# A scan's first pair, fetched and fronted inside the projections that precede it

## Chip, cores and metric

One core of one Trainium2 chip runs the whole program. The metric is device time in microseconds (us), the median of several executions; a profile of one more execution gives the trace.

## What is computed

Two encoder layers over 512 tokens of width 1024, in float32. Each layer is a half-step SwiGLU feed-forward, a token mixer, and a second half-step feed-forward, each followed by a residual and a layer norm. The mixer of layer 0 is neighbourhood attention, that of layer 1 a bidirectional RWKV-7 scan, and the change lies at the border inside this second mixer, between its projections and its scan. Cut to what matters there:

```
xr, xw, xk, xv, xa, xg = (x + xx * mix[i] for i in range(6))
r = xr @ w_rkv[0];  k = xk @ w_rkv[1];  v = xv @ w_rkv[2]
decay = exp(-exp(-softplus(-wl) - 0.5))         # wl: w0 + tanh(xw @ w1) @ w2, for two directions z
a = sigmoid(a0 + (xa @ a1) @ a2)                # for two directions z
g = sigmoid(xg @ g1) @ g2
step: state = state * w_t + (state @ a_t) b_t + v_t k_t;  out = state @ r_t
return ((y + bonus) * g) @ w_out
```

## The kernel before

**Stages.** Three feed-forwards and the attention come first, then `rwkv_project` (the projections), then the scan (`Scan`), then the last feed-forward. Matmuls that need float32 precision are made of three passes over a high and a low part (`mm3`, L225 to L227); `split` makes the parts, the high one on ACT (L220) and the low one on DVE or POOL (L221).

**Projections.** `rwkv_project` keeps the raw activations of all tokens in one tile `xraw` (pool `xr`). `mixed(i)` makes the split mix for a projection, `raws(i, dst)` the unsplit mix, which goes to DRAM. `decays(z)` computes the log-decays of direction z (eight matmul groups, eight stores into `d_lw`). The last loop makes the gate: per channel block c six matmuls from `gh` and `ug`, one ACT copy out of PSUM (L628) and one store into `d_g`. Its results pass through eight slots of a ring. The matrix of receptances r is made for the first block alone; xr and xv go to DRAM for the scan to use.

**Scan.** Heads are worked in eight pairs hp, tokens in eight chunks, directions in z = 0, 1. `load(hp)` fetches k, the inverse norms iv and a2 of a pair. `front(hp, z)` fetches r and the log-decays `lw`, sums them over tokens with four matmuls against a triangular constant `tri` (L1212, into bank "a"), takes two exponentials (L1215, L1217), makes the second LoRA product with `ah` and `a2u` (mm3 in bank "a"), a tanh (L1222) and, on DVE, the scaled operands `ar` and `bk`. `grams(hp, z)` multiplies `bk` by `ar` for four chunks at a time (L1271), masks the product into a unit tile `xs` on DVE (L1276), and then, for each of two heads, copies three pieces of `xs` on ACT (`qd`, `qc`; L1280, L1282) and moves two halves by DMA:

```
nc.scalar.activation(p.qc[h * 64 : h * 64 + 32, us, :], x[r : r + 32, h, :, 0, 32:64], AF.Copy)
nc.sync.dma_start(az[own, h], x[own, h, :, 1, :])
nc.sync.dma_start(x[own, h], ar[hs, ss])
```

The last of these overwrites what the ACT copy reads, so it waits for that copy. `receptances` (thread "r") loads the eight blocks of xr (into `az` and two units `xs`), the weights of r for pair 1 (into a unit `xs`), the eight blocks of `xv`, then more weights, and computes r for pairs 1 to 7 in groups of eight matmul rows (L982, banks "y" and "m"). `outs` (thread "o", from slot 6 on) loads rows of `w_out` into tiles that have come free, `w[0]` to `w[7]`, and adds up the output projection of the first five pairs: steps for i = 0, 1, 2, 3, 4 in this order.

**Order.** In the scan PE, ACT and DVE run in the order in which the code issues their work, and a table `SEQ` interleaves the threads of each slot. In the projections only PE's order is that of the code; the other engines' is planned by a timeline model when the program is built. All DMAs go out from SP's queue, whose order is planned too. Slot -2 begins `g0 v f1 f1 f1 f1 f1 f1 g0 l g0 r r`: a gram group of (0, 0), then front (0, 1), then the first receptance steps.

**Pools.** `rwb` holds the scan's tiles and opens when the projections' pools close; `rwe` on the right holds those tiles (`EARLY_TAGS`) that must be free before the last slot.

Of the kernel before, what the change touches and what calls it, by code (L numbers as in the profile page):

```python
# [10 lines left out]
F32 = mybir.dt.float32  # L11
# [61 lines left out]
EARLY = 5  # L73
EARLY_TAGS = ("k", "iv", "r", "lw", "kz", "a2r", "a2u", "v", "vr", "qc", "qd", "zs", "qs", "tm")
DECAY = math.exp(-0.5)
# [23 lines left out]
class Trunk:  # L99
# [78 lines left out]
    def bank(self, tag="bank"):  # L178
        return self.ps.tile([P, 512], F32, name=tag, tag=tag, bufs=self.banks.get(tag))

# [388 lines left out]

    def rwkv_project(self, dram, xraw, w_rkv, w1, w2, a1, g1, g2, heads):  # L570

        nc = self.nc
        with self.pool("rwa") as pool:
            with self.behind(self.mid):
# [73 lines left out]
            with self.tc.manual_schedule(engines=MANUAL):  # L648
# [55 lines left out]
                u = self.load_cols(g1, 0)  # L704
                u2 = pool.tile([P, 2, ND, 32], F32R, name="g1b")
                raw = self.tmp()[:, : ND * 32].rearrange("p (c f) -> p c f", c=ND)
# [270 lines left out]
class Scan:  # L977
# [5 lines left out]

    def __init__(self, k, pool, dram, consts, a2, w_r, w_v, w_out):
        self.k, self.nc, self.pool, self.dram, self.a2, self.w_r, self.w_v, self.w_out = k, k.nc, pool, dram, a2, w_r, w_v, w_out
        nc = self.nc
        self.opened = ExitStack()
        early = self.early = self.opened.enter_context(k.pool("rwe", "right"))
        self.first = {}
        self.tri = early.tile([P, 2, P], F32, name="tri")  # L990
        self.mask = early.tile([P, 2, 2, CH], F32, name="mask")
        self.onesb = early.tile([P, P], F32, name="onesb")
        self.eye = consts["eye"]
        self.ah = early.tile([P, 2, S], F32R, name="ah")
        self.xv = pool.tile([P, ND, S], F32, name="xv")
        self.consts = consts
# [17 lines left out]
        self.free = list(range(NBUF))  # L1014
        self.taken, self.st, self.py = {}, {}, {}

# [3 lines left out]
    def tile(self, tag, shape, bufs=1, dtype=F32):  # L1020
        if tag in self.first:
            return self.first.pop(tag)
        pool = self.early if tag in EARLY_TAGS else self.pool
        return pool.tile(shape, dtype, name=tag, tag=tag, bufs=bufs)
# [54 lines left out]
    def run(self, late, lead, ln):  # L1079
        with self.k.tc.manual_schedule(engines=MANUAL_SCAN):  # L1080
            raw = self.tile("e", [P, S], 2)
            for dst, src in ((raw, self.dram["ah"]), (self.tri, self.consts["tri"])):
                self.nc.sync.dma_start(dst, src)
# [3 lines left out]
            for n in ("mask", "onesb"):  # L1087
                self.nc.sync.dma_start(getattr(self, n), self.consts[n])
            self.zs = []
# [90 lines left out]
    def load(self, hp):  # L1180
# [11 lines left out]
        k.split(p.a2u[:, 0], p.a2u[:, 1], raw)  # L1192
        p.pc = tile_("pc", [P, NC, 2], 4)
        p.qd = tile_("qd", [P, NU, 32], 2)
        p.qc = tile_("qc", [P, NU, 32], 2)
        p.az = self.az[hp % 3]
        p.units, p.ar, p.bk = [], [], []
        yield

    def front(self, hp, z):  # L1200
# [7 lines left out]
        lw = tile_("lw", [P, NT, P], 2)  # L1208
        nc.sync.dma_start(lw, self.dram["lw"][:, z, :, hp * P : (hp + 1) * P])
        pi = k.bank("a")  # L1210
# [11 lines left out]
        nc.scalar.activation(th, pa, AF.Tanh, scale=0.5, bias=k.col(C_A0H + z, hp))  # L1222
        ar = tile_("ar", [P, NC, 2, CH], 2)
        bk = tile_("bk", [P, NC, 2, CH], 2)
        at, rt = ar[:, way, 0, :], ar[:, way, 1, :]
# [14 lines left out]
        if z == 0:  # L1240
            nc.vector.scalar_tensor_tensor(p.iv, p.k, k.col(C_KKH, hp), p.iv, ALU.mult, ALU.mult)
        kz = tile_("kz", [P, S], 2)
        nc.scalar.activation(kz, th, AF.Identity, scale=k.col(C_KA1, hp), bias=k.col(C_KA2, hp))
# [219 lines left out]
    def outs(self):  # L1463
# [114 lines left out]
def trunk_kernel(tc, x, ffn_w_in, ffn_w_out, ln_g, ln_b, cols, w_qkv, b_qkv, bias, mask, w_o, b_o,  # L1578
                 w_rkv, w1, w2, a1, a2, g1, g2, rw_out, heads, tri, smask, onesb, eye, out):
    nc = tc.nc  # L1580
    with ExitStack() as ctx:
# [12 lines left out]
        with k.activations(), k.psum(bank=8), k.weights(3):  # L1594
# [11 lines left out]
            with ExitStack() as xs:  # L1606
                with k.behind(*k.last):
                    xraw = k.ffn(xT, ffn_w_in[1, 0], ffn_w_out[1, 0], 3, lambda: XRaw(k, xs.enter_context(k.pool("xr"))))
                k.store_x(grid(dram["x"]))
                k.rwkv_project(dram, xraw.x, w_rkv, w1, w2, a1, g1, g2, heads)  # L1610
        with ExitStack() as late:
            with k.pool("rwb") as pool:
                scan = Scan(k, pool, dram, dict(tri=tri, mask=smask, onesb=onesb, eye=eye), a2, w_rkv[0], w_rkv[2], rw_out)
                with k.psum(a=2, g=2, p=1, c=1, m=1, y=1):
# [78 lines left out]
```

## Time and profile before

| what | value |
|---|---|
| median of 3 runs | 2267.66 us (2266.18 to 2270.35) |
| the profiled execution, its own time | 2262.09 us |
| its span, its mean granted PE clock | 2260.3 us, 0.984 |
| PE, weight loads (PEld) busy | 2169.9 us (96%), 1707.2 us (76%) |
| DVE, ACT, POOL busy | 1084.6 us, 974.6 us, 1423.4 us |
| DMA queue of SP | 326.58 MB, 45.9% of 16 engines' span |

The projections' last matmul ends at about 1442.6 us of the span and the last feed-forward follows the scan at about 1900 us. PE is busy nearly everywhere; what matters is where it is not. In the rows that follow, each row of a timeline has the start, the duration, the engine, line, operation, output and inputs, the count of merged instructions and, in brackets, the idle time before it with the instruction that ended it.

### The profile page before, as it was taken

The page shows a single profiled execution, that of the slowest core. Times are in us where ns is not written, and L with a number is a line of the kernel's source. Part 1 is how long each engine was busy: PE and PEld are TensorE (multiplying, and loading weights), DVE is VectorE, ACT ScalarE, POOL GpSimd, SP SyncE. Part 2 cuts the span into 40 slices and gives each one's busy share as a digit, 9 for nine tenths or more (in the row PEclk, how much of TensorE's full clock was granted, in tenths as well). Part 3 has the DMA queues.
Part 4 walks back from the last instruction along what each step waited for, and adds up shares of the span by engine and source line. Part 5 has one row for each costly group of instructions (what it writes and reads, how often), then busy time and mean ns, then how long its engine had stood idle before and what let it go on. Part 6 is the DMA issues. An engine that isn't in the chain of part 4 may idle for free. (4 is left out here: it accounts for less than half of the span.)

```text
span 2260.3 us, 35130 instructions
## 1 busy us (share of the span) xinstructions
PE 2169.9 (96%) x13784; PEld 1707.2 (76%) x13784; DVE 1084.6 (48%) x1549; ACT 974.6 (43%) x1706; POOL 1423.4 (63%) x1237
## 2 busy tenths in 40 slices
PE   8999999999999999999999988799999898999998
PEld 7888878887888888788888775435666556888886
DVE  2333356376423333743333698435787535233346
ACT  4333335376333333533333436336777533333334
POOL 6878855554487886588777433144776712888763
PEclk9999999999999999999999999899999999999999
DMA  7444463432344445354444534864444542444443
GB/s 204 143 149 145 140 214 101 134 89 91 103 140 149 144 141 181 123 176 140 140 140 134 192 122 143 275 165 132 134 125 119 181 149 85 158 144 140 145 168 121
DMA packets 350497, 328.82 MB, mean 145 GB/s; under 512 B 48458, under 2 KB 277450, under 8 KB 350332
## 3 DMA queue, kind: packets, MB, share of 16 engines
q1 hardware_dynamic: 350332, 326.58, 45.9%
q8 instruction: 108, 1.77, 0.3%
q14 instruction: 57, 0.47, 0.1%
HBM read 262.26 MB, written 47.74 MB: 137 GB/s over the span
## 5 line engine op out<-in xcount | busy, mean ns | idle before, releaser
L221 POOL TENSOR_TENSOR w<-raw,w 128x1024 fp32r<-128x1024 f32 (+2 forms) x203 | 501.5, 2472 | 253.6 <-ACT w L220 240.1
L226 PE MATMUL bank<-xT,w 128*128 128x512 f32 x1416 | 551.8, 390 | 1.7 <-DVE xT L221 1.7
L225 PE MATMUL bank<-xT,w 128*128 128x512 f32 x1416 | 552.9, 390 | 0.0
L227 PE MATMUL bank<-xT,w 128*128 128x512 f32 x1416 | 551.5, 389 | 0.0
L220 ACT ACTIVATE w<-raw 128x1024 fp32r<-128x1024 f32 x207 | 218.4, 1058 | 327.9 <-POOL ts L768 138.0
L422 DVE SCALAR_TENSOR_TENSOR ar<-bank,tmp 128x512 f32<-128x512 f32 x88 | 60.9, 692 | 580.7 <-PE bank L227 566.2
L226 PEld LDWEIGHTS bank<-xT,w 128*128 128x128 f32 x1416 | 266.1, 188 | 56.6 <-DVE xT L221 2.6
L227 PEld LDWEIGHTS bank<-xT,w 128*128 128x128 f32 x1416 | 266.0, 188 | 54.9
L225 PEld LDWEIGHTS bank<-xT,w 128*128 128x128 f32 x1416 | 266.0, 188 | 54.0
L797 PE MATMUL bank<-w,ring 128*128 128x512 f32 x864 | 201.5, 391 | 11.0 <-DVE w L221 10.1
L797 PEld LDWEIGHTS bank<-w,ring 128*128 128x128 f32 x864 | 161.6, 188 | 48.3 <-DVE w L221 13.1
L797 PE MATMUL bank<-wx,an 128*128 128x512 f32 x792 | 187.3, 389 | 0.0
L1360 POOL TENSOR_TENSOR tm<-qs,zs 128x126 f32<-128x126 f32 (+22 forms) x248 | 105.5, 425 | 125.7 <-DVE qs L1353 77.3
L797 PEld LDWEIGHTS bank<-wx,an 128*128 128x128 f32 x792 | 148.8, 188 | 30.8
L221 POOL TENSOR_TENSOR wx<-ra,wx 128x512 fp32r<-128x512 f32 x132 | 166.8, 1291 | 3.5 <-ACT wx L220 2.4
L221 DVE TENSOR_TENSOR ring<-ar,ring 128x1024 fp32r<-128x1024 f32 x44 | 130.0, 2955 | 76.0 <-ACT ring L220 75.9
L420 ACT ACTIVATE tmp<-bank 128x512 f32<-128x512 f32 x88 | 52.6, 598 | 225.8 <-PE bank L227 225.7
L221 POOL TENSOR_TENSOR ring<-raw,ring 128x1024 fp32r<-128x1024 f32 x28 | 69.7, 2499 | 105.6 <-ACT ring L220 105.6
L1362 POOL TENSOR_TENSOR zs<-zs,tm 128x126 f32<-128x126 f32 (+22 forms) x248 | 112.2, 452 | 19.4
L221 POOL TENSOR_TENSOR w<-late,w 128x1024 fp32r<-128x1024 f32 x28 | 71.3, 2547 | 75.9 <-ACT w L220 68.9
L220 ACT ACTIVATE wx<-ra 128x512 fp32r<-128x512 f32 x132 | 82.9, 633 | 72.4 <-PE bank L797 67.9
L225 PE MATMUL bank<-xT,ring 128*128 128x256 f32 (+1 forms) x352 | 104.5, 304 | 9.5 <-ACT xT L220 3.4
(285 smaller groups left out, 3730.5 us busy)
## 6 DMA issues: line engine op xcount, KB each, us to landing
raw<-in_ffn_w_in_dram SPq DMA_DIRECT2D x176, 512.0 KB, 3.7
ra<-in_ffn_w_out_dram SPq DMA_DIRECT2D x44, 1024.0 KB, 4.9
late<-d_late SPq DMA_DIRECT2D x30, 512.0 KB, 6.0
late<-in_ffn_w_out_dram SPq DMA_DIRECT2D x28, 512.0 KB, 4.4
raw<-in_w_qkv_dram SPq DMA_DIRECT2D x24, 512.0 KB, 3.8
d_late<-ts SPq DMA_DIRECT2D x44, 256.0 KB, 3.1
d_late<-ra SPq DMA_DIRECT2D x44, 256.0 KB, 2.0
xs<-ar SPq DMA_DIRECT2D x64, 128.0 KB, 2.3
```

The costliest lines, as they stand in the source:

```text
L220: self.hi = self.nc.scalar.activation(h, raw, AF.Copy).ins
L221: self.lo = (eng or self.nc.vector).tensor_tensor(l, raw, h.bitcast(F32), ALU.subtract).ins
L225: nc.tensor.matmul(out, wh, xh, start=start, stop=False)
L226: nc.tensor.matmul(out, wh, xl, start=False, stop=False)
L227: nc.tensor.matmul(out, wl, xh, start=False, stop=stop)
L420: nc.scalar.activation(s, pg, AF.Silu)
L422: nc.vector.scalar_tensor_tensor(raw[:, 3:7:3] if j else raw[:, 0:8:7], halves_of(pu), 0.5, halves_of(s), ALU.mult, ALU.mult)
L797: self.nc.tensor.matmul(acc, lhs, u[:, i], start=bool(first) and m == 0, stop=last and m == 2, skip_group_check=more)
L1360: nc.gpsimd.tensor_tensor(tv, qs[:, s, 0:s].rearrange("p (a o) -> p a o", o=1).broadcast_to([P, s, n]), zs[:, s : s + 1, c0:].broadcast_to ...
L1362: nc.gpsimd.tensor_tensor(zs[:, 0:s, c0:], zs[:, 0:s, c0:], tv, ALU.add)
```

## The change

The front of pair 0, direction 0, moves from the head of the scan into the last loop of `rwkv_project`. The raw mix (`raws(3)`) is made ahead of `decays(1)`, the pool of `xraw`, now on the right side, closes there, and a pool `rws` opens in its place (and beyond it) for `tri`, `mask`, `onesb`, `ah` and the front's tiles. `begin` fetches all of them; the front's `lw` matmuls stand before the gate loop, its second product after the gate's first block. Four spare quarters of a ring tile hold `raw`, `e`, `e2` and `th`. `ar`, `bk` and `kz` get one tile per direction instead of two in turn. With `az[2]` in `rwb`, `outs` puts `w[1]` and `w[2]` into its halves, `w[3]` into `bk1` and `w[4]` into `ar1`.

```diff
+START_TAGS = ("k", "iv", "r", "lw", "kz0", "ar0", "bk0", "a2r", "a2u", "pcs")
+EARLY_TAGS = ("kz1", "v", "vr", "qc", "qd", "zs", "qs", "tm")
...
+                list(raws(3, dram["xv"]))
+                xs.close()
+                scan.begin()
                 decays(1)
-                list(raws(3, dram["xv"]))
+                scan.fetch(0, 1)
+                start = scan.front(0, 0)
+                next(start)
+                next(start)
                 ug = [self.load_rows(g2, 0), self.load_unit(g2[P:, :])]
                 for c in range(ND):
...
                     store(dram["g"][:, c, :], pp)
+                    next(start, None)
...
+    def begin(self):
+        pool = self.start = self.opened.enter_context(self.k.pool("rws", "right"))
...
+        for dst, src in ((raw, self.dram["ah"]), (self.tri, self.consts["tri"])):
+            nc.sync.dma_start(dst, src)
+        load = self.load(0)
+        next(load)
+        self.fetch(0, 0)
+        self.k.split(self.ah[:, 0, :], self.ah[:, 1, :], raw)
+        next(load)
+        for n in ("mask", "onesb"):
+            nc.sync.dma_start(getattr(self, n), self.consts[n])
...
-        self.az = [(early if i == 2 else pool).tile([P, 2, NU, CH], F32, name=f"az{i}") for i in range(3)]
+        self.az = [pool.tile([P, 2, NU, CH], F32, name=f"az{i}") for i in range(3)]
...
-            raw = self.tile("e", [P, S], 2)
-            for dst, src in ((raw, self.dram["ah"]), (self.tri, self.consts["tri"])):
-                self.nc.sync.dma_start(dst, src)
-            list(self.load(0))
-            self.k.split(self.ah[:, 0, :], self.ah[:, 1, :], raw)
-            list(self.front(0, 0))
...
-        w += [self.tile(n, [P, NC, 2, CH], 2).rearrange("p a b c -> p (a b c)") for n in ("ar", "ar", "bk", "bk")]
+        w += [self.az[2][:, i].rearrange("p a b -> p (a b)") for i in range(2)]
+        w += [self.tile(n, [P, NC, 2, CH]).rearrange("p a b c -> p (a b c)") for n in ("bk1", "ar1")]
```

In the built programs the change moves instructions as follows; the line numbers of after are higher by 2 to 31.

PE at the end of the projections, before: the last three gate matmuls, the front of (0, 0), its first gram group (merged rows), and the front of (0, 1) up to the first receptance group.

```order
L227 MATMUL bank<-ring,w 128x512
L1212 MATMUL a<-tri,lw 128x128 x4
L225 MATMUL a<-ah,a2u 128x512
L226 MATMUL a<-ah,a2u 128x512
L227 MATMUL a<-ah,a2u 128x512
L1271 MATMUL g<-ar,bk 128x128 x8
L1212 MATMUL a<-tri,lw 128x128 x4
```

The same engine after, from the last matmul of `decays(1)` (bank<-w,ring) through the gate's first block of six (bank<-ring,w) to the beginning of its second:

```order
L229 MATMUL bank<-w,ring 128x512
L1243 MATMUL bank<-tri,lw 128x128 x4
L227 MATMUL bank<-ring,w 128x512
L228 MATMUL bank<-ring,w 128x512
L229 MATMUL bank<-ring,w 128x512
L227 MATMUL bank<-ring,w 128x512
L228 MATMUL bank<-ring,w 128x512
L229 MATMUL bank<-ring,w 128x512
L227 MATMUL bank<-ah,a2u 128x512
L228 MATMUL bank<-ah,a2u 128x512
L229 MATMUL bank<-ah,a2u 128x512
L227 MATMUL bank<-ring,w 128x512
```

The `lw` matmuls of (0, 0) now stand ahead of the whole gate loop, and the second product between its first and second block; after the loop follow the grams, then the front of (0, 1), then the receptances, as before.

SP's queue at the border, before: the loads of the scan's first tiles after the gate stores, then the loads of the receptances in one run up to the first weights (`xs<-in_w_rkv`).

```order
L629 DMA d_g<-ring 128x512 x7
L1083 DMA tri<-in_tri_dram 128x256
L1185 DMA k<-d_k 128x512
...
L1207 DMA r<-d_r 128x512
L1209 DMA lw<-d_lw 128x4x128
...
L1189 DMA a2r<-in_a_dram 128x2x128
L1038 DMA az_10811<-d_xr 128x512 x4
L1038 DMA xs_10807<-d_xr 128x512 x2
L1038 DMA xs_10798<-d_xr 128x512 x2
L1043 DMA xs_10783<-in_w_rkv_dram 128x8x128
```

The same queue after (the row above the first is the last store of `raws(3)`); `az_10858`, `xs_10845` and `ar_10742` are the pieces of the first gram group.

```order
L1012 DMA tri<-in_tri_dram 128x256
...
L1228 DMA lw<-d_lw 128x4x128
...
L631 DMA d_g<-ring 128x512 x7
...
L1333 DMA wv<-in_w_rkv_dram 128x8x128
L1067 DMA az_10860<-d_xr 128x512
L1313 DMA az_10858<-xs_10845 64x4x64 x2
L1067 DMA az_10860<-d_xr 128x512 x3
L1314 DMA xs_10845<-ar_10742 64x512 x2
L1067 DMA xs_10856<-d_xr 128x512 x2
L1067 DMA xs_10847<-d_xr 128x512 x2
L1072 DMA xs_10832<-in_w_rkv_dram 128x8x128
```

The first loads have moved ahead of the gate stores; the receptances' loads now have four transfers of the first gram group among them (two `az<-xs`, two `xs<-ar`).

SP's queue at slot 6, before: the loads of `w_out`; the first load, of `w[1]` into `ar`, and that of `w[3]` into `bk` stand well ahead of the other five.

```order
L1473 DMA ar<-in_rw_out_dram 128x1024
...
L1473 DMA bk<-in_rw_out_dram 128x1024
...
L1484 DMA xs_10781<-in_rw_out_dram 128x1024
L1482 DMA bk<-in_rw_out_dram 128x1024
L1484 DMA xs_10783<-in_rw_out_dram 128x1024
L1473 DMA ar<-in_rw_out_dram 128x1024
L1473 DMA wv<-in_rw_out_dram 128x1024
L1521 DMA bon<-d_bon 128x512
```

The same place after, all seven loads in one run: `w[3]` in `bk1`, `w[0]` in `wv`, and `w[1]` and `w[2]` in the halves of `az`.

```order
L1504 DMA bk_15800<-in_rw_out_dram 128x1024
L1504 DMA wv<-in_rw_out_dram 128x1024
L1515 DMA xs_10830<-in_rw_out_dram 128x1024
L1513 DMA ar_15801<-in_rw_out_dram 128x1024
L1515 DMA xs_10832<-in_rw_out_dram 128x1024
L1552 DMA bon<-d_bon 128x512
L1504 DMA az_10860<-in_rw_out_dram 128x1024
L1353 DMA d_bon<-bon 128x512
L1504 DMA az_10860<-in_rw_out_dram 128x1024
```

`w[0]`, which PE needs first, moves from fifth of the run to second; `w[1]`, needed next, moves from long before the run to its sixth load.

More of the change, by code (lines that the diff above doesn't have):

```diff
@@ L178, in bank @@
     def bank(self, tag="bank"):
-        return self.ps.tile([P, 512], F32, name=tag, tag=tag, bufs=self.banks.get(tag))
+        tag = tag if tag in self.banks else "bank"
+        return self.ps.tile([P, 512], F32, name=tag, tag=tag, bufs=self.banks[tag])
     def load_unit(self, src, chunks=None, ring=False, eng=None):
@@ L567, in na_residual, with rwkv_project @@
             yield
-    def rwkv_project(self, dram, xraw, w_rkv, w1, w2, a1, g1, g2, heads):
+    def rwkv_project(self, dram, xraw, w_rkv, w1, w2, a1, g1, g2, heads, xs, scan):
         nc = self.nc
-        with self.pool("rwa") as pool:
+        if True:
             with self.behind(self.mid):
@@ L704, in rwkv_project @@
                 u = self.load_cols(g1, 0)
-                u2 = pool.tile([P, 2, ND, 32], F32R, name="g1b")
+                u2 = flat2(self.ring())[0][:, : 2 * ND * 32].rearrange("p (i c f) -> p i c f", i=2, c=ND)
                 raw = self.tmp()[:, : ND * 32].rearrange("p (c f) -> p c f", c=ND)
@@ L982, in wide, with __init__, open @@
             self.nc.tensor.matmul(out[hs], w[:, hs], x, start=start, stop=stop)
-    def __init__(self, k, pool, dram, consts, a2, w_r, w_v, w_out):
-        self.k, self.nc, self.pool, self.dram, self.a2, self.w_r, self.w_v, self.w_out = k, k.nc, pool, dram, a2, w_r, w_v, w_out
-        nc = self.nc
[L987 to L994, printed above, removed]
+    def __init__(self, k, dram, consts, a2, w_r, w_v, w_out):
+        self.k, self.nc, self.dram, self.a2, self.w_r, self.w_v, self.w_out = k, k.nc, dram, a2, w_r, w_v, w_out
+        self.opened, self.consts = ExitStack(), consts
+        self.first, self.lws = {}, {}
+        self.free = list(range(NBUF))
+        self.taken, self.st, self.py = {}, {}, {}
+    def begin(self):
+        nc = self.nc
+        pool = self.start = self.opened.enter_context(self.k.pool("rws", "right"))
+        self.tri = pool.tile([P, 2, P], F32, name="tri")
+        self.mask = pool.tile([P, 2, 2, CH], F32, name="mask")
+        self.onesb = pool.tile([P, P], F32, name="onesb")
+        self.ah = pool.tile([P, 2, S], F32R, name="ah")
+        ring = self.k.ring(F32)
+        raw, *rest = (ring[:, i * S : (i + 1) * S] for i in range(4))
+        self.first.update(zip(("e", "e2", "th"), rest))
+        for dst, src in ((raw, self.dram["ah"]), (self.tri, self.consts["tri"])):
[7 more added lines that the diff above has]
+            nc.sync.dma_start(getattr(self, n), self.consts[n])
+    def open(self, pool):
+        self.pool = pool
+        early = self.early = self.opened.enter_context(self.k.pool("rwe", "right"))
+        self.eye = self.consts["eye"]
         self.xv = pool.tile([P, ND, S], F32, name="xv")
-        self.consts = consts
         unit = lambda i: (pool.tile([P, 2, 4, 2, CH], F32, name=f"xs{i}"), pool.tile([P, 2, 4, CH], F32, name=f"tb{i}"))
@@ L1008, in __init__ @@
         self.units = [units[i] for i in range(NBUF)]
-        self.az = [(early if i == 2 else pool).tile([P, 2, NU, CH], F32, name=f"az{i}") for i in range(3)]
+        self.az = [pool.tile([P, 2, NU, CH], F32, name=f"az{i}") for i in range(3)]
         for i in range(2):
             self.clear(i)
-        self.free = list(range(NBUF))
-        self.taken, self.st, self.py = {}, {}, {}
+        self.room(0)
     def place(self, tag, shape, bufs=1):
@@ L1192, in load, with room, fetch @@
         k.split(p.a2u[:, 0], p.a2u[:, 1], raw)
-        p.pc = tile_("pc", [P, NC, 2], 4)
-        p.qd = tile_("qd", [P, NU, 32], 2)
-        p.qc = tile_("qc", [P, NU, 32], 2)
+        p.pc = tile_("pc", [P, NC, 2], 4) if hp else tile_("pcs", [P, NC, 2])
+        p.units, p.ar, p.bk = [], [], []
+        if hp:
+            self.room(hp)
+        yield
+    def room(self, hp):
+        p = self.st[hp]
+        p.qd = self.tile("qd", [P, NU, 32], 2)
+        p.qc = self.tile("qc", [P, NU, 32], 2)
         p.az = self.az[hp % 3]
-        p.units, p.ar, p.bk = [], [], []
-        yield
+    def fetch(self, hp, z):
+        lw = self.lws[hp, z] = self.tile("lw", [P, NT, P], 2)
+        self.nc.sync.dma_start(lw, self.dram["lw"][:, z, :, hp * P : (hp + 1) * P])
     def front(self, hp, z):
@@ L1207, in front @@
             nc.sync.dma_start(p.r, self.dram["rkv"][0][:, hp, :])
-        lw = tile_("lw", [P, NT, P], 2)
-        nc.sync.dma_start(lw, self.dram["lw"][:, z, :, hp * P : (hp + 1) * P])
+        if (hp, z) not in self.lws:
+            self.fetch(hp, z)
+        lw = self.lws.pop((hp, z))
         pi = k.bank("a")
```

17 lines of the change are left out of this document (7 added, 10 removed).

## The prediction

> **What bounds the kernel now.** I read the page first, then PE's timeline at the border of projections and scan, then SP's and ACT's timelines for what PE waits for there, then the table by windows for the clock, and last the place in slot 6 where the moved tiles are used. The page says that PE is the bound:
>
> ```profile
> PE 2169.9 (96%) x13784; PEld 1707.2 (76%) x13784; DVE 1084.6 (48%) x1549; ACT 974.6 (43%) x1706; POOL 1423.4 (63%) x1237
> ```
>
> So only time in which PE waits, or runs at a lower clock, can be won or lost. PE's timeline at the border (the last matmul of `decays(1)`, the first and last of the gate, the front of (0, 0), the first grams, the end of the front of (0, 1), the first receptances, the second grams):
>
> ```profile
> 1428.10 0.39 PE L227 MATMUL bank<-w,ring 65*128 65x512 f32 x1
> 1428.32 0.40 PE L225 MATMUL bank<-ring,w 128*128 128x512 f32 x1
> ...
> 1442.24 0.39 PE L227 MATMUL bank<-ring,w 32*128 32x512 f32 x1
> 1450.12 2.04 PE L1212 MATMUL a<-tri,lw 128*128 128x128 f32 x8 [7.48 <-DMA mask<-in_smask_dram]
> 1452.70 0.79 PE L225 MATMUL a<-ah,a2u 128*128 128x512 f32 x1 [0.54 <-ACT ah L220]
> ...
> 1459.49 2.08 PE L1271 MATMUL g<-ar,bk 64*128 64x128 f32 x16 [4.84 <-DVE bk L1249]
> ...
> 1464.22 0.63 PE L227 MATMUL a<-ah,a2u 128*128 128x512 f32 x1
> 1465.76 3.65 PE L982 MATMUL y<-az,xs 128*64 128x512 f32 x16 [0.91 <-DMA xs<-in_w_rkv_dram]
> 1469.34 1.16 PE L1271 MATMUL g<-ar,bk 64*128 64x128 f32 x16
> ```
>
> PE waits 7.48, 0.54, 4.84 and 0.91 us, 13.77 us in all, between 1442.63 and 1465.76. That is all that the move can win. Three stretches of the table by windows (columns: busy time of PE, PEld, DVE, ACT and POOL, granted PE clock, DMA share, GB/s) show two more facts:
>
> ```profile
> 1444.00:1446.00 2.00, 0.00 (x0) 0.00 (x0) 0.00 (x0) 0.00 (x0) 0.00 (x0) 0.60 0.86 264
> 1464.00:1466.00 2.00, 1.09 (x4) 0.32 (x5) 1.48 (x3) 1.77 (x5) 0.00 (x0) 0.78 1.05 359
> 1466.00:1555.00 89.00, 89.00 (x633) 38.57 (x629) 33.68 (x53) 40.73 (x100) 28.15 (x69) 1.00 0.61 168
> ```
>
> The clock falls to a half within the wait and is back only at about 1464.9. And from 1466 to 1555 PE has no idle time at all: whatever moves the first receptance matmul moves all of this, one for one. The first receptance matmul is the mark on which I settle the account.
>
> **The first new wait: the front's `lw`, ahead of the gate.** PE runs in order, and its first front matmuls now stand ahead of the whole gate loop, so they are wanted at 1428.3. They need `tri` and `lw`, which SP's queue issues behind the last `d_xv` store, since the tiles lie where `xraw` was:
>
> ```profile
> 1432.67 0.60 SPq L636 DMA_DIRECT2D d_xv<-tmp  x1
> 1433.36 8.46 SPq L629 DMA_DIRECT2D d_g<-ring  x7
> 1441.91 0.38 SPq L1083 DMA_DIRECT2D tri<-in_tri_dram  x1
> 1446.15 0.43 SPq L1209 DMA_DIRECT2D lw<-d_lw  x1
> ```
>
> ```profile
> lw<-d_lw SPq DMA_DIRECT2D x1, 256.0 KB, 3.9
> ```
>
> DVE's order up to that store is unchanged, so `tri` goes out when the first `d_g` did, at 1433.4, a gain of 8.5 us for the fetch. From `tri` to `lw` the queue took 4.24 us; `r` and one `d_g` that stood between are now elsewhere, for which I take off 1.5 us: issue at 1436.1, landing 3.9 us later (the second fence, the DMA view of that one issue: KB, us from issue to landing), at 1440.0. PE waits 11.7 us where it had worked without a break. If nothing comes off, it is 1441.5.
>
> **What the gate loop then covers.** Prices at full clock, from the same operations later:
>
> ```profile
> 1494.78 1.06 PE L1212 MATMUL a<-tri,lw 128*128 128x128 f32 x8
> 1502.78 0.50 PE L225 MATMUL a<-ah,a2u 128*128 128x512 f32 x1
> ...
> 1503.35 0.40 PE L227 MATMUL a<-ah,a2u 128*128 128x512 f32 x1
> ```
>
> The gate took 1428.32 to 1442.63, 14.31 us; `lw` 1.06 and the second product 0.97 make 16.34 us. After an 11.7 us wait PE starts at half clock. How long that lasts after a restart is seen best in slot 6, where PE restarts at 1797.72 and the window 1802 to 1803 has a clock of 0.60, so that it is back at 1802.8:
>
> ```profile
> 1802.00:1803.00 1.00, 1.00 (x10) 0.40 (x8) 0.00 (x0) 0.00 (x0) 0.84 (x3) 0.60 0.00 0
> ```
>
> ```profile
> 1797.72 1.98 PE L982 MATMUL a<-wv,xv 128*64 128x512 f32 x4 [5.79 <-DMA wv<-in_rw_out_dram]
> ```
>
> That is 5.1 us at half speed, a loss of 2.55 us. The gate ends at 1440.0 + 16.34 + 2.55 = 1458.9. The DVE and ACT work of the front lies beside seven gate blocks of 1.79 us, so `bk` is ready and the waits of 7.48, 0.54 and 4.84 us are gone; if that cover failed, the 4.84 us would come back. The grams start at 1458.9 instead of 1459.49. At full clock grams (1.16), `lw` (1.06) and second product (0.97) end at 1462.1 instead of 1464.85: 2.75 us won. So the whole move wins little, because the wait for the fetch has only moved ahead of the gate.
>
> The Trainium skill, TensorE: Matmul & The Clock Gate, section Part 1: The HAM clock gate, says that PE stays at half rate until about 3.4 us of activity fill a free-running window; by that, as an estimate, each restart costs between 1.7 and 3.4 us, and the two restarts that I count leave the sum between 1.7 us lower and 1.7 us higher.
>
> **The second new wait: the receptances' loads.** They stand in the same queue behind the gate stores, and now have two `az<-xs` and two `xs<-ar` of the first gram group among them. An instruction of this queue that waits holds all behind it. The `xs<-ar` pair waits for ACT's copies of the masked grams, and these stand on ACT behind the front of (0, 1):
>
> ```profile
> 1466.06 0.81 ACT L1243 ACTIVATE kz<-th,cols 128x512 f32<-128x512 f32 x1
> 1466.78 0.61 ACT L1280 ACTIVATE qd<-xs 32x128 f32<-32x128 f32 x2
> ...
> 1468.37 0.31 ACT L1282 ACTIVATE qc<-xs 32x128 f32<-32x128 f32 x1
> ```
>
> ```profile
> 1457.21 1.92 SPq L1038 DMA_DIRECT2D xs<-d_xr  x4
> 1459.17 0.43 SPq L1043 DMA_DIRECT2D xs<-in_w_rkv_dram  x1
> 1486.86 1.20 SPq L1284 DMA_DIRECT2D xs<-ar  x2
> ```
>
> The second `qc` ended at 1468.68, 3.83 us after the second product of (0, 1); after, that is 1462.1 + 3.83 = 1465.9. Then follow the second `xs<-ar` (0.6), four xr blocks (1.92) and the weights for pair 1: issue at 1468.4, where it was 1459.17 before. Held behind it are also xv, wanted by the values thread. How long the weights take to land lies between two rows:
>
> ```profile
> xs<-in_w_rkv_dram SPq DMA_DIRECT2D x1, 512.0 KB, 6.5
> raw<-in_ffn_w_in_dram SPq DMA_DIRECT2D x176, 512.0 KB, 3.7
> ```
>
> 6.5 us is this same load in the full DMA traffic of before, 3.7 us the median of loads of its size elsewhere. The queue stood still before it, but a megabyte of xr goes just ahead; I take 5.5 us, nearer the first. The first receptance starts at 1473.9 instead of 1465.76: 8.1 us late. PE has waited since 1462.1, so the clock is halved again where it was full before, another 2.55 us. The mark is 10.7 us late, and the 89 us without idle time pass this on.
>
> The Trainium skill, DMA: Bandwidth & Descriptors, section Anatomy of one DMA, gives a fit of 2.0 us plus the bytes at 436 GB/s for loads issued from GpSimd; by it, as an estimate, 512 KB land in 3.2 us and the sum is 2.3 us smaller.
>
> **Slot 6.** The loads of `w_out` before, in SP's timeline, then the landing of the first and the last of the run, then PE's second step:
>
> ```profile
> 1771.69 0.43 SPq L1473 DMA_DIRECT2D ar<-in_rw_out_dram  x1
> 1786.90 0.55 SPq L1484 DMA_DIRECT2D xs<-in_rw_out_dram  x1
> 1789.05 0.59 SPq L1473 DMA_DIRECT2D wv<-in_rw_out_dram  x1
> ```
>
> ```profile
> wv<-in_rw_out_dram SPq DMA_DIRECT2D x1, 512.0 KB, 8.6
> xs<-in_rw_out_dram SPq DMA_DIRECT2D x1, 512.0 KB, 3.7
> ```
>
> ```profile
> 1800.69 1.97 PE L982 MATMUL a<-ar,xv 128*64 128x512 f32 x4
> ```
>
> Five loads go out from 1786.90, the first lands in 3.7 us and the fifth, `w[0]`, at 1797.65: 1.76 us for each further one. PE waits 5.79 us for it, and takes `w[1]` 2.97 us later. After, `w[0]` is second and lands at 1792.4, half a microsecond after PE wants it (1797.72 - 5.79 = 1791.9); but `w[1]` is now the sixth, with one load of half its size ahead of it: 1797.65 + 1.76 + 0.9 = 1800.3, and PE waits there. It starts 0.4 us sooner than at 1800.69, but with 5.1 us at half clock ahead of it instead of 2.1, worth up to 1.5 us, of which I count 0.9, since part of the work there is chain steps that wait for ACT and DVE; with the 0.4 us that makes 0.5 us lost. The ends: 8.3 us won, if neither weight is waited for and the clock stays up (5.79 + 2.55); 2.6 us lost, if the second half of `az` is late by another load of 1.76 us plus the half one.
>
> **Edits without a term.** `ar`, `bk` and `kz` had two buffers in turn and now have one per direction, which alternate in the same way. `g1b` in a ring tile, `pcs` and the earlier `raws(3)` leave DVE's and POOL's order as it was. In the gate loop ACT has the stores and the front; eight ring slots keep the stores from holding it. None of these touches a PE wait by the rows above; if one did, it would show as a wait in the gate.
>
> **Sum.** 8.1 + 2.55 + 0.5 = 11.2 us. The profiled execution (2262.09 us, span 2260.3) would become 2273.3. The median of the runs is 5.57 us above that execution, so the predicted median is 2267.66 + 11.2 = 2278.9 us.
>
> **Rivals.**
> Slot 6 pays back: `w[1]` lands in time, since traffic in SP's queue ahead of the run is thinner by two loads. For it: `w[0]` surely comes sooner. Against: more bytes go out in the same run. With 4 to 8.3 us won there the time is 2270 to 2274. Chance 0.20.
> The queue does not hold what stands behind a waiting transfer. Then the receptances' loads go out beside the gate, the first receptance starts at 1462.1 at full clock, 3.7 us earlier than before, and the time is 2264, not slower. It decides if the weights for pair 1 go out before 1460. Against it is SP's own wait row, in which stores wait for ACT while `tri`, which waits for none of them, stands behind:
>
> ```profile
> SPq L629 <- ACT ring L628: 5.6, 6, 1.4
> ```
>
> Chance 0.07.
> The fetches are slower: `lw` at 1441.5, the weights in 6.5 us, 2.6 us in slot 6: 1.5 + 1.0 + 2.1 more, 2283.5. Chance of as much or more 0.10. My forecast, 2274 to 2283, has 0.63.
>
> **How the numbers follow.** About 0.2% (4.5 us) is what a measurement of this kernel can tell from no change. Slower by more: the forecast, the slow rival and half of the first rival, 0.83. Within: the other half and part of the second, 0.13. Faster: the rest, 0.04. The range leaves out the second rival and the last few us of the slow one: 2270 to 2284.
>
> **What would show it.** PE idle of about 12 us ended by a DMA ahead of the `lw` matmuls, before the gate; none ahead of the first grams; about 12 us ahead of the first receptance group, ended by `xs<-in_w_rkv`, whose issue follows the second `qc`; clock 0.5 after both. In slot 6, no wait of note at `wv` and one at `az`. The forecast is wrong if the weights go out before the `qc` copies end, or if `lw` lands before 1436.

## The result and the profile after

The kernel after takes 2279.26 us (median of 5 runs, 2276.23 to 2282.18), the kernel before 2269.08 us beside it (5 runs, 2266.18 to 2270.53). The ratio is 1.0046, with a 95% interval from 1.0031 to 1.0060: slower by 10.2 us. The profiled execution of after took 2276.78 us, with a granted PE clock of 0.980 where it was 0.984.

Busy times of the page of after:

```profile
PE 2173.2 (96%) x13784; PEld 1709.6 (75%) x13784; DVE 1087.8 (48%) x1549; ACT 974.3 (43%) x1706; POOL 1423.8 (63%) x1237
```

The matmuls are as many as before; PE is 3.3 us busier on them, at a lower mean clock. The rest is waiting. PE's timeline of after at the border (the end of `decays(1)`, the front of (0, 0), the end of the gate, first grams, end of the front of (0, 1), first receptances, second grams):

```profile
1432.08 0.39 PE L229 MATMUL bank<-w,ring 65*128 65x512 f32 x1
1445.10 2.04 PE L1243 MATMUL bank<-tri,lw 128*128 128x128 f32 x8 [12.63 <-DMA lw<-d_lw]
...
1462.10 0.39 PE L229 MATMUL bank<-ring,w 32*128 32x512 f32 x1
1462.42 1.16 PE L1301 MATMUL g<-ar,bk 64*128 64x128 f32 x16
...
1464.98 0.40 PE L229 MATMUL a<-ah,a2u 128*128 128x512 f32 x1
1481.97 5.50 PE L991 MATMUL y<-az,xs 128*64 128x512 f32 x16 [16.60 <-DMA xs<-in_w_rkv_dram]
1487.40 1.16 PE L1301 MATMUL g<-ar,bk 64*128 64x128 f32 x16
```

The zero of time has to be set first: `decays(1)` ended at 1432.47 here and at 1428.49 in the profile of before, 3.98 us earlier, although PE's order up to there is the same in both. The experiments show that executions differ by nearly as much: run 3, which is the kernel before up to there, has this end at 1430.26, and the runs on after, without the two that move the raw mix, have it between 1429.35 and 1432.28. Whether a part of the 3.98 us is the change's own (`raws(3)` now stands ahead of `decays(1)`) isn't settled by these. So all marks below are counted from the end of `decays(1)`. In these terms the first grams start at 29.95 us (before: 31.0), the first receptance at 49.50 (37.27) and the second grams at 54.93 (40.85). The two waits of before behind the gate (7.48 and 4.84 us) are gone, and two new ones of 12.63 and 16.60 us have come.

SP's timeline of after shows why the second is so long, and its table of waits which transfer was held by what (us in total, times, the longest):

```profile
1436.65 0.60 SPq L638 DMA_DIRECT2D d_xv<-tmp  x1
1437.34 0.60 SPq L1012 DMA_DIRECT2D tri<-in_tri_dram  x1
...
1440.50 0.60 SPq L1228 DMA_DIRECT2D lw<-d_lw  x1
...
1449.92 11.75 SPq L631 DMA_DIRECT2D d_g<-ring  x7
...
1465.22 1.37 SPq L1313 DMA_DIRECT2D az<-xs  x2
1466.64 1.59 SPq L1067 DMA_DIRECT2D az<-d_xr  x3
1471.66 1.13 SPq L1314 DMA_DIRECT2D xs<-ar  x2
1472.84 2.21 SPq L1067 DMA_DIRECT2D xs<-d_xr  x4
1475.11 0.42 SPq L1072 DMA_DIRECT2D xs<-in_w_rkv_dram  x1
```

```profile
SPq L631 <- ACT ring L630: 11.7, 8, 2.3
SPq L1314 <- DMA az<-xs: 3.3, 1, 3.3
```

`lw` goes out as soon as the last `d_xv` store and a handful of loads are through, and is late for PE. The gate, which waited with PE, gives its stores late; the stores hold the queue; behind them the `xs<-ar` pair holds it for another 3.3 us, and the weights go out at 1475.11 and land 6.86 us later, when PE starts. The table by windows for after (columns as in the prediction) shows what the DMA engines did meanwhile:

```profile
1446.00:1464.00 18.00, 18.00 (x77) 10.83 (x76) 4.50 (x7) 7.67 (x14) 2.07 (x4) 0.94 0.51 169
1464.00:1472.00 8.00, 1.37 (x10) 0.89 (x8) 5.15 (x9) 4.64 (x12) 0.00 (x0) 0.79 0.98 263
1472.00:1482.00 10.00, 0.03 (x2) 0.06 (x2) 0.00 (x0) 0.00 (x0) 0.00 (x0) 0.50 0.89 260
```

While PE worked off the gate they were half idle (0.51); when PE had nothing left, they were nearly full (0.98 and 0.89). In slot 6, PE of after:

```profile
1810.96 1.97 PE L991 MATMUL a<-wv,xv 128*64 128x512 f32 x4 [0.89 <-DMA wv<-in_rw_out_dram]
1817.68 1.98 PE L991 MATMUL a<-az,xv 128*64 128x512 f32 x4 [3.67 <-DMA az<-in_rw_out_dram]
1821.25 1.98 PE L991 MATMUL a<-az,xv 128*64 128x512 f32 x4
1825.28 1.03 PE L991 MATMUL g<-wv,xv 128*64 128x512 f32 x4
```

`g<-wv` is 392.81 us after `decays(1)`, and was 378.01 (1806.50 in before): 14.80 us late where the second grams were 14.08 us late. Slot 6 up to here costs 0.7 us.

### The profile page after: what moved, and what is told of

It reads as the page before. It is cut to its first block, busy times and chain, and to the rows that moved or that the text cites. A ratio compares the mean times of both kernels' runs of the same rounds, so it can differ in the third digit from the quotient of the medians.

```text
span 2274.7 us, 35138 instructions
## 1 busy us (share of the span) xinstructions
PE 2173.2 (96%) x13784; PEld 1709.6 (75%) x13784; DVE 1087.8 (48%) x1549; ACT 974.3 (43%) x1706; POOL 1423.8 (63%) x1237
## 4 chain that ended last, share of the span: by engine, by line
PE 82%; DVE 8%; DMA 4%; ACT 3%; issue 2%; SPq 1%; POOL 0%; DVEq 0%; ACTq 0%; POOLq 0%
PE bank L227 16%; PE bank L228 16%; PE bank L229 16%; PE bank L806 14%; PE bank L290 4%; PE a L991 2%; PE y L991 1%; DMA wv<-in_w_rkv_dram 1%; DVE x L450 1%; PE g L1301 1%; DVE w L223 1%; DVE tmp L605 1%; DMA late<-in_ffn_w_out_dram 1%; PE m L991 1%; PE bank L1168 1%
## 5 line engine op out<-in xcount | busy, mean ns | idle before, releaser
L227 PE MATMUL bank<-xT,ring 128*128 128x256 f32 (+2 forms) x360 | 107.8, 307 | 9.8 <-ACT xT L222 3.9
```

What stands on the lines that cost most here:

```text
L227: nc.tensor.matmul(out, wh, xh, start=start, stop=False)
```

## The experiments

In the diffs `behind(x)` is a helper of the kernel that lets the enclosed instructions be issued only after x. Each kernel was timed with the kernel before beside it: 2267.94 us (27 runs) in the first four, 2267.43 (16) in the next four, 2268.43 (11) in the ninth, 2265.36 (11) in the last two.

**1. The weights ahead of the first gram group's transfers.** On after:

```diff
+            next(self.rs)
+            self.weights = self.fetched
...
+                with self.k.behind(*([self.weights] if hp + z + q == 0 else [])):
                     nc.sync.dma_start(az[own, h], x[own, h, :, 1, :])
                     nc.sync.dma_start(x[own, h], ar[hs, ss])
```

> The kernel after, with the four transfers of the first gram group (az<-xs, xs<-ar) queued on SP behind the first receptances' loads (xr blocks and the weights for pair 1); nothing else moves. Theory (the queue holds the weights behind transfers that wait for ACT and for a landing): the weights go out about 7.5 us earlier than in after, PE's wait ahead of the first receptance falls from 16.6 to about 9 us and the time by 7 to 7.6 us, to about 2272. The time before the first receptance, PE's wait for lw (12.6 us) and slot 6 stay as in after. Rival (the weights are late because the DMA traffic there is full, the queue's order hides nothing): issue earlier, landing as much longer, and the time falls by 0 to 2 us.

Measured: 2273.02 us (12 runs), ratio to before 1.0029 (1.0016 to 1.0042); 6.2 us below after by the medians, 3.9 by the two ratios, whose intervals overlap. SP's and PE's timelines:

```profile
1467.73 0.43 SPq L1072 DMA_DIRECT2D xs<-in_w_rkv_dram  x1
```

```profile
1442.43 2.05 PE L1246 MATMUL bank<-tri,lw 128*128 128x128 f32 x8 [12.38 <-DMA lw<-d_lw]
1474.22 6.47 PE L991 MATMUL y<-az,xs 128*64 128x512 f32 x16 [11.41 <-DMA xs<-in_w_rkv_dram]
```

From the end of `decays(1)` (1430.05 here) the weights go out at 37.7 us, 5.0 earlier than in after, and PE starts at 44.17, 5.3 earlier. The landing took 6.5 us, hardly less than 6.86: an earlier issue was an earlier landing. So the queue's order cost some 5 us, not the 7 to 7.6 that I had expected; xr itself had still to wait behind the last gate store.

**2. The front begun late in the gate loop.** On after:

```diff
                 start = scan.front(0, 0)
-                next(start)
-                next(start)
...
-                    next(start, None)
+                    if c == 6:
+                        next(start)
+                        next(start)
+                    if c > 6:
+                        next(start, None)
+                list(start)
```

> The kernel after, with the front of (0, 0) begun only behind block 6 of the gate loop instead of ahead of it (its second product behind block 7, the rest behind the loop). Theory (the cost is one of the place in PE's order: the fetch of lw is waited for because nothing stands ahead of it): PE's wait at lw falls from 12.6 us to 0 to 1, a wait of up to 5 us for bk ahead of the first grams comes back, the first gram group and the weights' issue come 9 to 12 us earlier, the first receptance about as much, up to 18 us if the clock also stays full there: 2258 to 2270, below the kernel before if the gain is over 10 us. Rival (the pool's layout, the one buffer per direction or slot 6 costs the time): the wait at lw goes, but another comes in its place and the time stays at 2275 or above.

Measured: 2262.95 us (12 runs), ratio 0.9979 (0.9968 to 0.9989): 16.3 us below after. PE, and a row of the table by windows:

```profile
1441.71 1.13 PE L1246 MATMUL bank<-tri,lw 128*128 128x128 f32 x8
1450.82 2.08 PE L1304 MATMUL g<-ar,bk 64*128 64x128 f32 x16 [5.48 <-DVE bk L1282]
...
1465.47 5.12 PE L994 MATMUL y<-az,xs 128*64 128x512 f32 x16 [9.84 <-DMA xs<-in_w_rkv_dram]
1470.52 1.16 PE L1304 MATMUL g<-ar,bk 64*128 64x128 f32 x16
```

```profile
1452.00:1472.00 20.00, 10.16 (x55) 5.65 (x53) 5.82 (x10) 4.64 (x12) 1.10 (x3) 0.67 1.08 323
```

The wait for `lw` is gone; it was one of place. The grams come at 21.47 us, 9.5 earlier than in before. But the second grams come at 41.17, and before had 40.85: what the front wins, the wait for the weights takes back to the last 0.3 us. The new theory: the loads of the receptances set this mark, since they can only start behind the gate's stores and then keep the DMA engines full (the row by windows: share 1.08 from 1452 to 1472).

**3. `w[0]` first in slot 6 of the kernel before.** The w_out loads, other than `w[0]` and `w[1]`, stand in `with self.k.behind(first)`, where first is the load of `w[0]`.

> The kernel before, with the loads of w_out in slot 6 in another order: w[0] (wv<-w_out) first, the other early ones behind it. Theory (a late load there halts PE, and the clock with it): the wait of 5.79 us at the first matmul of slot 6 goes, the clock stays up there, and the time falls by 5 to 8 us, to 2260 to 2264. Rival (traffic, not order: whichever load comes second is as late): PE waits about as long at w[1], gain 0 to 2 us. The run also executes all of the program up to the scan as the kernel before does, so it shows how much two executions of the same code differ at the border.

Measured: 2259.68 us (6 runs), ratio 0.9959 (0.9945 to 0.9972): 8.3 us below before. PE starts slot 6 without a wait:

```profile
1794.41 1.11 PE L982 MATMUL a<-wv,xv 128*64 128x512 f32 x1
...
1797.52 1.14 PE L982 MATMUL a<-ar,xv 128*64 128x512 f32 x4
```

`g<-wv` comes at 372.16, 5.85 us earlier than in before, as the theory had it. This gain has no need of the moved front. The border is as in before, with its second grams at 41.3 us.

**4. Both 1 and 2.**

> The kernel after with both edits: the front begun behind block 6 of the gate, and the first gram group's transfers queued behind the weights for pair 1. Theory: the weights' issue then depends on neither the lw wait nor ACT's qc copies; no wait of over 3 us ahead of the first receptance, and the time 2 to 4 us below that of the late front alone. Rival (the gate stores and the DMA traffic hold the weights then): within 1 us of the late front alone.

Measured: 2263.12 us (10 runs), ratio 0.9979 (0.9968 to 0.9989): no gain over the late front, as the rival had it. The first receptance comes 2.1 us earlier (34.05), but its group takes 1.3 us longer at half clock, and the second grams come at 40.4, 0.7 us earlier.

**5. to 8. The order in slot 6, and an early raw mix.** Runs 5 and 6 let each of `w[1]` to `w[3]` stand behind the one ahead of it, and the rest behind `w[3]`, on run 2 and on after; run 7 makes `raws(3)` ahead of `decays(0)`, run 8 does both on after:

```diff
+            with self.k.behind(*last):
+                last = [nc.sync.dma_start(w[i], rows(self.w_out, i)).ins]
-            nc.sync.dma_start(w[i], rows(self.w_out, i))
```

```diff
                 mg = mixed(5)
+                list(raws(3, dram["xv"]))
                 decays(0)
...
-                list(raws(3, dram["xv"]))
                 xs.close()
```

> The late front of the second run, and in slot 6 the loads of w_out queued in the order in which PE takes them (w[0], w[1], w[2], w[3], then the rest). Theory: the border stays as in the second run, the wait of 5.34 us at az (w[1]) goes and the clock stays up there: 6 to 9 us below the late front alone, about 2254 to 2257. Rival (the loads are bound by traffic, so the last of the run is late whatever it is): a wait of 3 us or more moves to bk or az, gain 0 to 3 us.

Measured: 2259.48 us (8 runs), ratio 0.9968 (0.9956 to 0.9979): 3.5 us below run 2, not 6 to 9. This is the wait in run 2:

```profile
1802.75 1.98 PE L994 MATMUL a<-az,xv 128*64 128x512 f32 x4 [5.34 <-DMA az<-in_rw_out_dram]
```

In its place stand four of 0.63 and 0.68 us at az and 0.21 each at bk and ar, so 3.6 us of waiting are gone; `g<-wv` is 4.9 us earlier. The rest is clock: in run 2 it was 0.50 from about 1799.6 to 1806.4, in run 5 it stays at 1.00 there. The gain in clock came, but smaller than priced, and 1.7 us of waits came back.

> The kernel after, with only the order of the w_out loads in slot 6 changed (w[0], w[1], w[2], w[3], then the rest). Theory: the waits of 0.89 and 3.67 us at wv and az go, with them a stretch at half clock (1.6 to 2.6 us): 6 to 7 us below after, about 2272 to 2273; the border stays as in after. Rival (traffic): 0 to 3 us. The time of after less this time is all that slot 6 costs in after; the rest of after's loss against before is then the border's.

Measured: 2274.23 us (6 runs), ratio 1.0037 (1.0023 to 1.0051): 5.0 us below after by the medians, 2.0 by the ratios; counted from `decays(1)` to the end of the span it is 2.8 us (839.4, after 842.2), since waits of 1.16 and 0.55 us at az stay. With slot 6 mended, after is still 6.8 us slower than before, whose slot 6 is not. Against run 3, which has its own in order, it is 14.5 us slower by the medians, and its second grams come at 54.35 us where run 3 has 41.32: that is the border.

> The kernel after, with the raw mix (raws(3)) made ahead of decays(0) instead of ahead of decays(1); the front of (0, 0) keeps its place before the gate, and PE's order is that of after. The tiles where xraw lay are then free some 60 us earlier, and SP issues tri and lw ahead of the stores of decays(1). Theory (the wait of 12.63 us at lw is the fetch, which waits for the raw mix): it falls to 0 to 1, the gate ends 12 to 14 us earlier, no wait at the first grams; the first receptance then waits longer (15 us or more), since xr and the weights queue behind the gate stores and the first gram group: it comes 12 to 16 us earlier than in after, the time is 2263 to 2268. Rival (lw is late for another reason, or DVE makes decays late when the raw mix stands ahead of them): a wait of 5 us or more stays ahead of the gate or comes in the projections, time over 2270.

Measured: 2273.80 us (6 runs), ratio 1.0032 (1.0019 to 1.0044). The rival came true: PE waits 11.28 us in the projections now, in the first layer of the gate, for a weight that stands on SP's queue behind the `d_xv` stores, and `decays(1)` ends 13 to 17 us later than in the profiles of before and after. The load of this weight, behind seven of the stores, and the wait:

```profile
1419.01 9.06 SPq L638 DMA_DIRECT2D d_xv<-tmp  x7
1428.66 0.38 SPq L710 DMA_DIRECT2D tmp<-in_g_dram  x1
```

```profile
1431.66 0.63 PE L227 MATMUL bank<-xT,ring 128*32 128x512 f32 x1 [11.28 <-ACT ring L222]
```

But the border behind it tells what was asked. PE's timeline of run 7:

```profile
1445.06 0.40 PE L229 MATMUL bank<-w,ring 65*128 65x512 f32 x1
1445.30 1.06 PE L1243 MATMUL bank<-tri,lw 128*128 128x128 f32 x8
1461.12 1.16 PE L1301 MATMUL g<-ar,bk 64*128 64x128 f32 x16
...
1479.68 5.92 PE L991 MATMUL y<-az,xs 128*64 128x512 f32 x14 [15.61 <-DMA xs<-in_w_rkv_dram]
```

With `lw` there in time, the front ahead of the whole gate costs no wait, the grams come at 15.66 us, 15 us earlier than in before, and PE then stands for 15.61 us; the second grams come at 40.5.

> The early raw mix and the w_out order of slot 6 together, on after. Theory: the two gains add, 6 to 8 us below the early raw mix alone, about 2256 to 2261. Rival (they share a cause): less than 3 us below the better of the two.

Measured: 2270.99 us (8 runs), ratio 1.0020 (1.0010 to 1.0030): 2.8 us below run 7, where 6 to 8 had been expected; from `decays(1)` to the end of the span it is 3.7 us. The wait of 4.96 us in slot 6 goes; the clock gives little beside it, since in run 8 it was 0.50 there too, from about 1809.8 to 1813.2.

**9. to 11. The weights ahead of xr.** On run 5, the weights of pair 1 are loaded ahead of the xr blocks, which stand behind them in the queue, and the first gram group's transfers behind both. Run 10 is run 5 again and run 11 run 9 again, side by side.

```diff
-        for c in range(ND):
-            nc.sync.dma_start(xr[c], self.dram["xr"][:, c, :])
...
             load(hp, one(self.units[i][0]))
             if hp == 1:
+                with self.k.behind(self.fetched):
+                    for c in range(ND):
+                        self.fetched = nc.sync.dma_start(xr[c], self.dram["xr"][:, c, :]).ins
```

> The late front and the w_out order of slot 6, with the weights of r for pair 1 queued ahead of the eight xr blocks instead of behind them, and the first gram group's transfers behind both. Theory (the loads of the receptances, which go out only behind the gate stores and move 2.5 MB, set the first receptance, wherever the front stands): the weights land early, but the last xr block takes their place as what ends last; the second gram group comes 40 to 41 us after the end of decays(1), as in every run so far in which lw was not waited for, and the time is within 2 us of the late front with the w_out order, 2257 to 2261. Rival (the weights alone were late, for their place in the queue): the first receptance 5 to 8 us earlier, PE stays at full clock, the time about 2252 to 2255.

> The late front with the w_out order once more, on the same chip as the next. Both theories: 2257 to 2261; second gram group 41 us after the end of decays(1).

> The weights ahead of xr once more: its profile had won 7 us at the border and lost them again in waits for wv and xv of 2.4 to 2.5 us each, while its median was 4.3 us lower. Theory (the border's gain is real, the later waits belong to that one execution): 3 to 5 us below the run beside it, second gram group 34 us after the end of decays(1), at most one wait of over 2 us for wv. Rival (the bytes delayed at the border are waited for later, in every execution): within 1.5 us of the run beside it, the waits for wv and xv there again.

Measured: 2255.14 us (6 runs), ratio 0.9937 (0.9915 to 0.9959) for run 9; 2258.89 (8 runs), 0.9972 (0.9961 to 0.9983) for run 10; 2256.54 (5 runs), 0.9960 (0.9947 to 0.9973) for run 11. PE and the table by windows of run 9:

```profile
1452.99 2.08 PE L1308 MATMUL g<-ar,bk 64*128 64x128 f32 x16 [5.93 <-DVE bk L1286]
...
1460.00 5.35 PE L994 MATMUL y<-az,xs 128*64 128x512 f32 x16 [2.15 <-DMA az<-d_xr]
1465.28 1.16 PE L1308 MATMUL g<-ar,bk 64*128 64x128 f32 x16
1468.91 1.08 PE L994 MATMUL a<-xv,wv 128*64 128x512 f32 x4 [2.46 <-DMA xv<-d_xv]
...
1471.63 1.16 PE L1308 MATMUL g<-ar,bk 64*128 64x128 f32 x16
```

```profile
1452.00:1472.00 20.00, 14.39 (x77) 8.15 (x79) 7.73 (x13) 5.57 (x15) 2.07 (x4) 0.79 1.06 331
```

My theory fell here in its strong form: the second grams come at 34.2 us (33.9 in run 11), 6 us or more earlier than in any other kernel. The weights were late for their place behind 2 MB of xr; putting the gram group's transfers behind them had brought 0.7 us in run 4. But the DMA engines stay full (1.06), and bytes put off are waited for later: xv at once (2.46 us; 2.64 in run 11), so that the third grams come at 40.5 us in both, where runs 5 and 10 have 45.1 and 45.6. Later, ahead of the values, PE waits 2.42 us in run 9 for a load (wv), and 2.50 there and 2.48 in run 11 in waits that the trace puts down to ACT's `kz`; that these, too, come of bytes put off isn't shown. Of the 7 us at the border, 2.4 are left in the medians of runs 10 and 11, between the theory of run 11 (3 to 5) and its rival (within 1.5), and 4.3 in those of runs 5 and 9. Both pairs have the same sign, but the intervals of the ratios overlap, so the size stays open. This kernel is the fastest, 23 to 24 us below after and 9 to 13 us below the kernel before beside it.

## Why the prediction was right

The time forecast was 2278.9 us and came out as 2279.26. The two new waits stand where the forecast had them and are ended by the loads that it named, but that the sum agrees to 0.4 us is luck: the border cost 3.4 us more than priced, and 4.4 us for which there was no term came back behind it.

**The first wait** was priced at 11.7 us and took 12.63 (12.38 and 11.89 in runs 1 and 6); run 2 shows that it is the front's place in PE's order that makes it, run 7 that it is the fetch behind the raw mix.

**The half clock** was priced at 2.55 us for each restart and cost less. The windows of after:

```profile
1448.00:1449.00 1.00, 1.00 (x4) 0.48 (x3) 1.00 (x2) 0.57 (x3) 0.00 (x0) 0.91 0.76 200
...
1485.00:1486.00 1.00, 1.00 (x4) 0.26 (x2) 0.00 (x0) 0.00 (x0) 0.00 (x0) 0.64 1.11 369
```

From 1445.10 to about 1448.2, and from 1481.97 to about 1485.7, PE ran at half: 3.1 and 3.75 us, so 1.5 and 1.9 us lost. 5.1 us, read off in slot 6, was the long end. The Trainium skill, TensorE: Matmul & The Clock Gate, section Part 1: The HAM clock gate, has about 3.4 us of activity fill the window, and by that, as an estimate, a restart costs 1.7 to 3.4 us; the second restart agrees and the first lies just under it.

**The gate's cover** held: first grams at 29.95 us, forecast 30.4 (1458.9 less 1428.49), without a wait for `bk`.

**The second wait** is the step that was mis-sized. I had the weights go out when ACT's second `qc` was done and the loads ahead were through, at 1468.4 in before's time, and land in 5.5 us. They went out at 1471.1 (1475.11 less 3.98), 2.7 us later. ACT was not late: its second `qc` of after,

```profile
1469.17 0.31 ACT L1312 ACTIVATE qc<-xs 32x128 f32<-32x128 f32 x1
```

ends at 1465.5 in before's time, and the forecast had 1465.9. But `xs<-ar` also waits for the landing of `az<-xs`, which reads the same unit, and went out only at 1471.66 of after; I had priced only ACT's copy. And they landed in 6.86 us, so the row of 6.5 from the same place was the one to take. Together 4.1 us; with the cheaper clock the second grams are 14.1 us late instead of 10.7. The fit of the Trainium skill, DMA: Bandwidth & Descriptors, section Anatomy of one DMA, is for loads issued from GpSimd; the 3.2 us that I had estimated by it for these 512 KB do not hold for this load from SP's queue behind 2 MB of others, which took 6.86.

**Slot 6** was forecast at 0.5 us lost and lost 0.7: `w[0]` came 0.89 us late, `w[1]` was waited for 3.67 us, as the forecast had it.

**What I had not priced** is the end of slot 6. Before and after, PE:

```profile
1836.95 0.69 PE L1433 MATMUL c<-wr,az 64*64 64x64 f32 x8 [2.49 <-ACT az L1404]
```

```profile
1852.03 1.19 PE L1430 MATMUL p<-qd,qc 32*32 32x32 f32 x62
1854.16 0.24 PE L1430 MATMUL p<-qd,qc 32*32 32x32 f32 x2 [0.94 <-issue]
1854.34 0.45 PE L1463 MATMUL c<-wr,az 64*64 64x64 f32 x8
```

The stop there is 2.49 us in before and 0.94 in after. Behind the longer one the clock falls to a half; this is a window of before:

```profile
1837.00:1838.00 1.00, 1.00 (x10) 0.74 (x12) 0.00 (x0) 0.29 (x2) 0.00 (x0) 0.50 0.97 287
```

In after it stays at 1.00 there, and after wins 3.0 us between two `g<-wv` (20.65 us apart in before, 17.68 in after). The last section says what makes this stop; nothing in the edit aims at it. So the account from the end of `decays(1)` is 14.1 + 0.7 - 3.0 = 11.8 us, and 1.4 us come back in small pieces up to the end of the span: 10.4, and 10.2 by the medians.

**The rivals.** Slot 6 didn't pay back up to `g<-wv`. The queue does hold what stands behind a waiting transfer: run 1 takes that away and wins. The slow rival had nearly the right landing of the weights (6.5 us) and too much for slot 6 (2.6).

**What the move itself is worth.** With each kernel's slot 6 put in order, the late front (run 5, 2259.48 us, ratio 0.9968) and the kernel before (run 3, 2259.68, 0.9959) can't be told apart. With xr ahead of the weights in the queue, it matters little where the front stands: behind the gate (before, run 3), late in it (runs 2, 4, 5 and 10) or ahead of it with `lw` there in time (runs 7 and 8), the first receptance comes at 34.1 to 37.7 us. After the latest of these its group takes 3.6 us, after the earliest two, ahead of which PE has stood for 7.3 and 15.6 us, 6.3 to 6.4 us, most of it at half clock, so that the second grams come at 40.4 to 41.8 us all the same. The waits of 13.77 us that I called all that the move can win were not to be won by the move alone.

Runs 9 and 11 win 7 us there with the moved front and another order of the loads. The kernel before with the weights ahead of xr was not run. As an estimate from its rows, that order alone could bring it less than 1 us: PE's own work ahead of the first receptance ends there at 36.4 us (1464.85 less 1428.49), where the first receptance now starts at 37.27, and run 9 has it at 28.88. So the move seems to pay at the border only together with the loads' order.

## What to carry to other kernels

Work moved ahead of a stage has to have its operands there: ask when its fetch can go out, which here was set by the tiles it overlays, and put it behind as much independent work of an in-order engine as it takes. Before moving work to fill a wait, look whether the transfer that ends last after it depends on the move at all; here stores, then 2.5 MB of loads at full DMA share set the end, until the loads themselves stood in another order. In a queue that is in order, put first what is needed first, and price each transfer in it with all that it waits for, a landing as well as an engine.

## What had not been expected of the hardware

PE stops at one place of the program for which no operand accounts. In all thirteen profiles it follows the 11,656th, 11,657th or 11,658th matmul (the count of the table by windows up to there), at the end of slot 6: 2.49 and 2.44 us in the kernel before and in run 3, 0.44 to 1.28 us in after and its variants. In before the trace ascribes it to ACT's `az<-p`, but in after the same `c<-wr,az` started at 1854.34, ahead of that copy (1854.44), and the stop falls within a row of 64 equal matmuls. The Trainium skill, Runtime: NRT & Kernel Launch, section Instruction fetch mechanics, says that an engine's instructions are fetched in blocks by DMA and that crossing a block is mostly hidden. The traces agree on the blocks and show a crossing that isn't hidden. Every page has a queue for them among its DMA queues (packets, MB, share of 16 engines), with 16 KB a packet:

```profile
q8 instruction: 108, 1.77, 0.3%
```

By the packets' times in the traces, one of them starts 2.20 to 2.41 us before PE goes on, in all thirteen profiles (in before at 1834.60, PE goes on at 1836.95; in after at 1851.83 and 1854.16), however long the stop was. So PE goes on a fixed time after the packet starts, not after it stopped: the stop is most likely the wait for this fetch. Why the fetch starts so late here, and later in before than in after, stays open; no run was made to change it.
